# A hybrid decoder step: where the last block's down weights are loaded and split, and how the first block's second norm is put in order

## The chip, the cores and the metric

The kernel runs on one core of a Trainium2 chip. Its engines are TensorE (PE, with PEld for its weight loads), VectorE (DVE), ScalarE (ACT), GpSimd (POOL) and SyncE (SP), which issues the DMAs. The metric is the time of one execution on the device in microseconds (us), as the median of several runs. Lower is better.

## The reference

One layer of a decoder that mixes attention with a spatial gate, on 2048 prompt positions and on 8 sequences of 4 new positions each (the samples). In outline:

```python
z = rmsnorm(x, norm1_g) @ w_in            # 1024 -> q, k, v | u, v of the gate
att  = dilated_window_attention(q, k, v)  # 8 heads, three dilations, merged
gate = spatial_gate(layernorm(vg))        # chunks of 128 positions
x = x + concat(att, u * gate) @ w_out     # 1024 -> 1024
n = rmsnorm(x, norm2_g)
x = x + (silu(n @ w_gate) * (n @ w_up)) @ w_down   # 1024 -> 2816 -> 1024
y = rmsnorm(x, final_g)                   # and caches of the last keys and values
```

Everything is float32. The change lies in the second norm `n` and in the loads of `w_down`.

## The kernel before

**Tiles and blocks.** The prompt is 16 tiles of 128 tokens. A first part of the kernel (up to about 880 us) does the input projection, attention and gate. Behind it come three blocks of tiles: 0 to 5, 6 to 11, and 12 to 15 with the 32 sample rows. Each block does the output projection in two halves of 512 columns, adds the residual (`acc`), takes the second norm and runs the feed-forward part.

**Precision.** A float32 matrix product is made of three fast ones: each operand is split into a high half (ACT copies it to the type `fp32r`) and a low half (POOL or DVE subtract the high half from the source), and PE multiplies high by high, high by low and low by high. `split_sb` (lines 135 and 138) does this for a whole operand; `high` (L1545) and `low_half` (L1549) for the gate and up weights.

**The feed-forward part.** The 2816 hidden columns are 22 slices `f` of 128. For each slice a *unit* of seven products replaces the eight of gate and up (a scheme of the Strassen kind). `product` (L1597) runs one: 4 steps of 3 matmuls over all tokens of the block into a bank `ps_m`, operand `q` of the slice (`op`) against the normed tokens (`xh`, `xl`). The seven weight operands are made from the weights once, in the first block, and kept in DRAM (`ab_d`); the later blocks load them (`load_source`, L1504) into a ring of eight buffers `fr`. In the first block `load_quarter` (L1510) loads the raw quarters and `gained` (L1513) multiplies them with the norm's gain `g2c`.

**The down products.** The hidden values of two slices (an even and an odd one) are kept, and `down_unit` (L1664, matmuls at L1679) multiplies them with the down weights `dw` of both: 24 matmuls of 512 columns for each tile, into `ps_o`. They run within the next even unit, behind its products 3, 4 and 5. The down weights come by `load_down` (L1586, DMA at L1588, 512 KB) into `fd`, which is a single buffer, and by `split_down` into one of two pairs `dw`.

**What sets the order.** The schedule is manual: each engine runs its instructions in the order in which the code writes them, and SP's DMAs too, each waiting where its buffer is not free. `one(u, q)` writes product `q` of a unit and then what is to follow it: `prepare` of the next slice (the low half of operand `q - 1` on POOL, the high half of operand `q` on ACT, the load of source `q` of the slice after it on SP), `roll` (copies of the sample caches from DRAM to DRAM, L1258), and the down weights:

```python
if q == 2 and f:
    load_down(f)
elif q == (5 if f % 2 else 6):
    split_down(f)
```

So a slice's down weights are loaded behind product 2 of its own unit, and split behind product 5 (odd slices) or 6 (even slices). `later(n, fn)` puts a step off until `tick` has been called `n` times; products, halves of projection and `down_unit` tick.

**The first block's second norm.** `first_block` writes the second halves of the output projection for the tiles in the order 2, 0, 1, 3, 4, 5 (`second_unit`, L1373 to L1375, into `ps_o`). Behind each, `second_end` adds it to the residual and starts the norm: square and sum on ACT (`norm2_a`), one and two ticks later the root, the inverse root by a Newton step on DVE and the scaled copy `xn` on ACT (`norm2_b`), and 1 to 3 ticks after that `norm2_c`: eight transposes on PE into two banks (`norm2_t`, L1439, by default `ps_t`), copies and six sums and differences (`norm2_v`, `norm2_s`), and the split into `xh` and `xl`. In the later blocks `chain` (L1481) writes these steps of a tile together, with the previous tile's `norm2_v` and `norm2_s` in the gaps. The first unit of a block (slice 0) runs in two parts, tiles 0 to 3 and then the rest (`part = 4`). `s1`, printed as `s`, holds a tile's sum and root; `acc` of two numbers are two tiles.

Of the kernel before, what the change touches and what calls it, by code (L numbers as in the profile page):

```python
# [10 lines left out]
F32 = mybir.dt.float32  # L11
# [53 lines left out]
def hymba_step(ctx: ExitStack, tc: tile.TileContext, A: dict, O: dict):  # L65
# [1315 lines left out]
    def out_end(B, i, half, ps):  # L1381
        hs = slice(half * 512, (half + 1) * 512)
        if B.rows[i] == P:
            dve.tensor_add(B.acc[i][:, hs], B.acc[i][:, hs], ps)
        else:
            tmp = zn_tile()[0:SR]
            act.activation(tmp, ps[SR:2 * SR, :], AF.Copy)
            dve.tensor_add(B.acc[i][0:SR, hs], B.acc[i][0:SR, hs], ps[0:SR])
            dve.tensor_add(B.acc[i][0:SR, hs], B.acc[i][0:SR, hs], tmp)
# [90 lines left out]

    def chain(B, i, ps, ahead):  # L1481

        out_end(B, i, 1, ps)
        s1 = B.s1.pop(i)
        act.activation(place_of(B, i)[0][:, 4:8], B.acc[i][:, 512:1024].rearrange("p (s t) -> p s t", t=P), AF.Square,
                       accum_out=s1[:, 3:4])
        rms_b(s1, P, s1[:, 3:4])
        if ahead:
            sums = norm2_v(B, *ahead)
        r = rms_c(s1, P)  # L1490
        xn = square_tile()
        act.activation(xn, B.acc[i], AF.Copy, scale=r)
        if ahead:
            norm2_s(B, *ahead, sums)
        return xn
# [16 lines left out]

    def gained(f, q):  # L1513
        w_ = ab[f]["q", q]
        for k in range(4):
            kk = k + (0, 0, 4, 4)[q]
            act.activation(w_[:, k * P:(k + 1) * P], w_[:, k * P:(k + 1) * P], AF.Copy, scale=g2c[:, kk:kk + 1])
        j = (0, 3, 6, 2)[q]
        if j != 3:
            ab[f][j] = w_  # L1520
# [385 lines left out]
    def second_end(B, i, ps, put_off=2):  # L1906
        out_end(B, i, 1, ps)
        norm2_a(B, i, put_off)

    def first_block(B):  # L1910

        m2, m1 = acc_place(2), acc_place(4)
        split_early(B, 1, m1)
        split_early(B, 2, m2)
        B.place()
        load_cat(B, 0, KD - 1, KD)
        load_cat(B, 5, 0, KD)
        merge_load(h, 2)
        load_acc(B, 1)
        load_acc(B, 0)  # L1920
        half1_load(*range(KD))
        sync.dma_start(gain[0], dap(A["final_g"], 0, [[0, P], [1, D]]))
        plan.run(10 ** 9)
        split_early(B, 3)
        for n, what in ((2, [(merge, h, 2, pool), (merge, h, 3, pool), (split_cat, B, 0), (split_early, B, 4)]),
                        (4, [(merge_store, h, 2, 4)]), (5, [(open_end, B, 1)]),
                        (6, [(half1_split, B, 0, 1)]), (7, [(open_end, B, 0), (split_cat, B, 5)]),
                        (8, [(half1_split, B, 2, 3)]), (9, [(half1_split, B, 4, 5), (sources, B, 0, 0, 1, 2, 3)]),
                        (10, [(half1_split, B, 6, 7)]), (11, [(sources, B, 1, 0, 1, 2, 3)])):
            later(n, both, *what)  # L1930
        for i in (1, 2, 3):
            open_unit(B, i)
        open_part(B, 0, (KD - 1,), False, True)
        for i in (4, 5):
            open_unit(B, i)
        first_operands(B)

        p2 = second_unit(B, 2)
        for i in (2, 3):
            load_acc(B, i)  # L1940
        second_end(B, 0, second_unit(B, 0))
        open_end(B, 2)
        second_end(B, 2, p2, 3)
        p1 = second_unit(B, 1)
        for i in (4, 5):
            load_acc(B, i)
        second_end(B, 1, p1)
        p3 = second_unit(B, 3)
        open_end(B, 3)
        second_end(B, 3, p3)  # L1950
        for i in (4, 5):
            open_end(B, i)
        for i in (4, 5):
            second_end(B, i, second_unit(B, i), 1)

    def first_end(B, i):
        open_end(B, i)
# [51 lines left out]
    for bi, B in enumerate(blocks):  # L2009
        if bi == 0:  # L2010
            first_block(B)
        else:
            next_block(B, downs, finals)
        if B.last:
            hs4 = consts.tile([P, 4, 2 * SR], F32R, name="hs4", tag="cats")
        nb = None if B.last else blocks[bi + 1]

        part = 4
        units = [dict(f=f, a=0, b=B.nt) for f in range(NF)]
        if not B.last:  # L2020
            units[0:1] = [dict(f=0, a=0, b=part), dict(f=0, a=part, b=B.nt)]
        rows = list(range(len(B.rows)))
        last_h = {}

        def one(u, q):
            tick()
            product(B, u, q)
            f = u["f"]
            if u["b"] < B.nt:
                if bi == 0 and q in (0, 2):  # L2030
                    sources(B, 2, q, q + 1)
                return

            if f and q < 2:
                prepare(B, f, 7 + q)
            if f + 1 < NF:
                prepare(B, f + 1, q)
            if f + 2 < NF:
                if bi == 0 and f:
                    if q in (0, 2):  # L2040
                        sources(B, f + 2, q, q + 1)
                if bi == 0:
                    ahead_of(f + 2, q)
            elif nb:

                for s in {(0, 2): (0, 1), (0, 4): (2, 3), (1, 3): (4, 5), (1, 5): (6, 7)}.get((f + 2 - NF, q), ()):
                    load_wo(0, s, fraw)
                if f + 1 == NF and q > 0:
                    split_wo(nb, 0, q - 1, lambda s: op_tile())
            if f + 1 < NF and q in (1, 3, 5)[:(1, 3, 2)[bi]]:  # L2050
                roll(1)

            if q == 2 and f:
                load_down(f)
            elif q == (5 if f % 2 else 6):
                split_down(f)

        def downs_of(pair, a, b):
            for i in rows[a:b]:
                down_unit(B, i, pair)  # L2060

        for n, u in enumerate(units):
            u["n"] = n
            for q in range(7):
                one(u, q)
                if u["f"] % 2 == 0 and u["f"] > 0 and 3 <= q < 6:
                    downs_of((B.h[0], B.h[1]), *((0, 2), (2, 4), (4, 9))[q - 3])
        pair = (B.h[0], B.h[1])
# [112 lines left out]
```

## Time and profile before

| | |
|---|---|
| median of three runs | 2521.73 us (2508.28, 2521.73, 2523.93) |
| the profiled execution | 2527.26 us; its span in the trace 2525.4 us |
| granted TensorE clock, mean | 0.989 |
| PE / PEld busy | 2442.6 us (97%) / 2116.0 us (84%) |
| DVE / ACT / POOL busy | 1270.2 (50%) / 1130.9 (45%) / 1303.2 us (52%) |
| DMA | 365.07 MB read, 157.84 MB written, 207 GB/s over the span |

The span is the time from the first to the last instruction in the trace of one execution; the rest of that execution's time lies around it. Busy shares are of the span. Rows of a timeline begin with the start in us, the length in us and the engine; then come the line of the kernel, the operation, its output and input, and "xN" where N like instructions are drawn together. A bracket at the end tells how long the engine stood idle ahead of the instruction, and which instruction's end released it. "SPq" is the DMA queue of SP, where a row's start is the issue; a row of "DMA" is a transfer. The granted clock is the share of full speed that the chip allows TensorE.

### The profile page before, as it was taken

The numbers are of one execution on the slowest core, as the hardware profiler recorded it, in microseconds if no ns is written. First come the engines' busy times: TensorE is split into PE (matmuls) and PEld (weight loads), VectorE is DVE, ScalarE is ACT, GpSimd is POOL, SyncE is SP. The second block draws the span as 40 slices with busy tenths as digits, with TensorE's granted clock in tenths as the row PEclk, the third lists the DMA queues.
The fourth block names the chain that finished last, engine by engine and source line by source line (L and its number), as shares of the span: only waits on it lengthen the run. The fifth ranks groups of instructions, "written<-read, shape, count | busy, mean of one in ns | idle before, by whom it ended". The sixth has DMA issues, their size and how long they took to land.

```text
span 2525.4 us, 39104 instructions
## 1 busy us (share of the span) xinstructions
PE 2442.6 (97%) x14022; PEld 2116.0 (84%) x14022; DVE 1270.2 (50%) x2595; ACT 1130.9 (45%) x2449; POOL 1303.2 (52%) x1019
## 2 busy tenths in 40 slices
PE   8998999999999899999999999999999998999997
PEld 7877776668887678999999989999999978888986
DVE  4558582217776645444444465444444465444444
ACT  7324343226666556454554446233233255333334
POOL 2216441005778447676776626445355445556565
PEclk9999999999999899999999999999999999999999
DMA  9974845675554554555555363535445363555553
GB/s 294 280 230 148 259 127 175 200 253 175 182 168 131 142 191 154 167 175 179 155 194 166 128 218 134 188 136 199 170 169 203 117 223 126 175 200 178 197 174 132
DMA packets 292292, 455.36 MB, mean 180 GB/s; under 512 B 28711, under 2 KB 160984, under 8 KB 286980
## 3 DMA queue, kind: packets, MB, share of 16 engines
q1 hardware_dynamic: 285252, 440.82, 53.6%
q10 hardware_dynamic: 6848, 12.06, 1.7%
q8 instruction: 111, 1.82, 0.3%
q14 instruction: 81, 0.66, 0.1%
HBM read 365.07 MB, written 157.84 MB: 207 GB/s over the span
## 4 chain that ended last, share of the span: by engine, by line
PE 62%; POOL 6%; issue 6%; DVE 3%; DMA 3%; ACT 2%; SPq 0%; POOLq 0%; DVEq 0%; ACTq 0%
PE ps_o L1679 15%; PE ps_m L1608 9%; PE ps_m L1607 9%; PE ps_m L1606 9%; POOL op L1549 4%; PE ps_s L856 3%; PE ps_o L911 2%; PE ps_t L883 1%; PE ps_s L935 1%; PE ps_s L318 1%; PE ps_o L1373 1%; PE ps_o L1375 1%; PE ps_o L1374 1%; PE ps_m L1373 1%; PE ps_m L1375 1%
## 5 line engine op out<-in xcount | busy, mean ns | idle before, releaser
L1549 POOL TENSOR_TENSOR op<-fr,op 128x512 fp32r<-128x512 f32 x385 | 487.5, 1299 | 246.6 <-ACT op L1545 232.5
L1606 PE MATMUL ps_m<-xh,op 128*128 128x384 f32 (+3 forms) x1904 | 604.9, 318 | 0.7 <-DVE zn L1627 0.4
L1608 PE MATMUL ps_m<-xh,op 128*128 128x384 f32 (+3 forms) x1904 | 604.4, 317 | 0.0
L1607 PE MATMUL ps_m<-xl,op 128*128 128x384 f32 (+3 forms) x1904 | 603.9, 317 | 0.1
L1679 PE MATMUL ps_o<-dw,hw 128*128 128x512 f32 x2040 | 492.6, 396 | 20.4 <-POOL dw L138 12.6
L1679 PEld LDWEIGHTS ps_o<-dw,hw 128*128 128x128 f32 x2040 | 385.1, 190 | 106.3 <-POOL dw L138 16.5
L1606 PEld LDWEIGHTS ps_m<-xh,op 128*128 128x128 f32 x1904 | 360.2, 189 | 5.3 <-ACT xh L1450 0.7
L1607 PEld LDWEIGHTS ps_m<-xl,op 128*128 128x128 f32 x1904 | 360.0, 189 | 4.0 <-DVE xl L1462 0.4
L1681 DVE TENSOR_TENSOR acc<-acc,ps_o 128x512 f32<-128x512 f32 (+1 forms) x362 | 248.3, 687 | 226.8 <-PE ps_o L1679 226.8
L1608 PEld LDWEIGHTS ps_m<-xh,op 128*128 128x128 f32 x1904 | 359.9, 189 | 0.0
L1646 ACT ACTIVATE ps_t<-zn 128x384 f32<-128x384 f32 (+1 forms) x126 | 58.5, 465 | 500.7 <-DVE zn L1629 423.8
L138 POOL TENSOR_TENSOR dw<-fd,dw 128x1024 fp32r<-128x1024 f32 x66 | 158.5, 2401 | 204.2 <-ACT dw L135 194.0
L1545 ACT ACTIVATE op<-fr 128x512 fp32r<-128x512 f32 x396 | 233.8, 626 | 3.4 <-PE ps_m L1375 3.4
L318 PE MATMUL ps_s<-wh,xh 128*128 128x512 f32 x480 | 196.8, 410 | 6.0 <-ACT xh L135 6.0
L320 PE MATMUL ps_s<-wh,xl 128*128 128x512 f32 x480 | 189.0, 394 | 0.0
L319 PE MATMUL ps_s<-wl,xh 128*128 128x512 f32 x480 | 188.9, 394 | 0.0
L1549 POOL TENSOR_TENSOR op<-pair,op 128x512 fp32r<-128x512 f32 x63 | 81.3, 1298 | 113.7 <-ACT op L1545 109.3
L536 POOL TENSOR_TENSOR pr<-kv,qb 96x512 f32<-96x512 f32 x32 | 45.6, 1425 | 170.3 <-DMA kv<-in_cache_k_dram 86.1
L318 PEld LDWEIGHTS ps_s<-wh,xh 128*128 128x128 f32 x480 | 90.9, 189 | 48.5 <-issue 23.7
L1656 ACT ACTIVATE hw<-ps_t 128x384 fp32r<-128x384 f32 (+1 forms) x126 | 54.2, 449 | 157.7 <-DVE ps_t L1652 157.7
L927 POOL CAST sq<-k 128x512 fp32r<-128x512 f32 x32 | 34.1, 1066 | 164.8 <-PE ps_s L319 164.8
L1274 DVE TENSOR_TENSOR hw<-ps_t,hw 128x384 fp32r<-128x384 f32 (+1 forms) x120 | 59.3, 508 | 109.7 <-ACT hs L1660 57.0
(490 smaller groups left out, 4328.7 us busy)
## 6 DMA issues: line engine op xcount, KB each, us to landing
fr<-ab_d SPq DMA_DIRECT2D x308, 256.0 KB
fd<-in_w_down_dram SPq DMA_DIRECT2D x66, 512.0 KB
out_ks_dram<-in_cache_k_dram SPq DMA_DIRECT2D x56, 512.0 KB
out_vs_dram<-in_cache_v_dram SPq DMA_DIRECT2D x56, 512.0 KB
ab_d<-fr SPq DMA_DIRECT2D x88, 256.0 KB
qk_d<-pair SPq DMA_DIRECT2D x64, 256.0 KB
ab_d<-pair SPq DMA_DIRECT2D x63, 256.0 KB
kv<-in_cache_k_dram SPq DMA_DIRECT2D x64, 192.0 KB
```

The costliest lines, as they stand in the source:

```text
L138: (eng_lo or pool).tensor_sub(lo, src, hi.bitcast(F32))
L318: pe.matmul(o[j], xh[:, k, :], wh, start=(k == 0), stop=False)
L319: pe.matmul(o[j], xh[:, k, :], wl, start=False, stop=False)
L320: pe.matmul(o[j], xl[:, k, :], wh, start=False, stop=(k == KD - 1))
L856: pe.matmul(s[:, a:b_], d[q][:, qs], d["k"][:, t0:t0 + b_ - a], start=(z == 0), stop=(z == 1))
L1545: act.activation(ops[f, j][0], ab[f][j], AF.Copy)
L1549: (pool if f or j in POOL_LOW else dve).tensor_sub(lo_, ab[f][j], hi.bitcast(F32))
L1606: pe.matmul(out, wh[:, ks], xh[:, :, k], start=(k == 0), stop=False)
L1607: pe.matmul(out, wh[:, ks], xl[:, :, k], start=False, stop=False)
L1608: pe.matmul(out, wl[:, ks], xh[:, :, k], start=False, stop=(k == 3))
L1679: pe.matmul(ps[0:nr], l_, r_[:, cs], start=(z == 0 and y == 0), stop=(z == FC - 1 and y == len(pairs) - 1))
L1681: dve.tensor_add(B.acc[i][0:nr, cs], B.acc[i][0:nr, cs], ps[0:nr])
```

## The change

In the last block, the split of an odd slice's down weights moves from behind product 5 to behind product 3 of its unit, that of an even slice stays behind product 6, and the load of the next slice's down weights is written directly behind each split, where it was behind product 2 of the slice's own unit. In the first block, the norm steps put off by ticks are replaced by `chain`, in a written order of projections, chains and transposes; tiles 2 and 3 transpose into banks of `ps_m`, tiles 4 and 5 into banks of `ps_o`; the root's activation table is loaded by a small activation at the front; the first unit runs in parts of three tiles each; and the gain of the quarters of slices 0 and 1 is one multiplication on POOL in place of four activations on ACT. `part` in the second block stays 4.

```diff
     def chain(B, i, ps, ahead):
-        out_end(B, i, 1, ps)
-        s1 = B.s1.pop(i)
-        act.activation(place_of(B, i)[0][:, 4:8], B.acc[i][:, 512:1024]..., AF.Square,
-                       accum_out=s1[:, 3:4])
-        rms_b(s1, P, s1[:, 3:4])
+        if ps is not None:
+            out_end(B, i, 1, ps)
+        if i in B.s1:
+            ...
+        else:
+            s1 = fl.tile([P, 4], F32, name="s1", tag="s1", bufs=6)
+            act.activation(place_of(B, i)[0], B.acc[i]..., AF.Square, accum_out=s1[:, 0:1])
+            rms_b(s1, P)
...
     def gained(f, q):
         w_ = ab[f]["q", q]
-        for k in range(4):
+        if f < 2:
+            kk = (0, 0, 4, 4)[q]
+            w3 = w_.rearrange("p (k c) -> p k c", k=4)
+            pool.tensor_mul(w3, w3, g2c[:, kk:kk + 4].unsqueeze(2).broadcast_to([P, 4, P]))
+        for k in range(4 if f > 1 else 0):
             kk = k + (0, 0, 4, 4)[q]
             act.activation(w_[:, k * P:(k + 1) * P], w_[:, k * P:(k + 1) * P], AF.Copy, scale=g2c[:, kk:kk + 1])
...
+        two = lambda fn, *a: [lambda: fn(*a[0:1]), lambda: fn(*a[1:2])]
         p2 = second_unit(B, 2)
+        act.activation(fl.tile([P, 4], F32, name="s1", tag="s1", bufs=6)[:, 0:1], ident[:, 0:1], AF.Sqrt)
         for i in (2, 3):
             load_acc(B, i)
-        second_end(B, 0, second_unit(B, 0))
+        p0 = second_unit(B, 0)
         open_end(B, 2)
-        second_end(B, 2, p2, 3)
+        out_end(B, 2, 1, p2)
+        x0 = chain(B, 0, p0, None)
+        x2 = chain(B, 2, None, None)
         p1 = second_unit(B, 1)
         for i in (4, 5):
             load_acc(B, i)
-        second_end(B, 1, p1)
+        open_end(B, 3)
+        x1 = chain(B, 1, p1, (0, norm2_t(B, 0, x0)))
         p3 = second_unit(B, 3)
-        open_end(B, 3)
-        second_end(B, 3, p3)
         for i in (4, 5):
             open_end(B, i)
-        for i in (4, 5):
-            second_end(B, i, second_unit(B, i), 1)
+        x3 = chain(B, 3, p3, (2, norm2_t(B, 2, x2, two(ps_m, 1, 2))))
+        p4 = second_unit(B, 4)
+        x4 = chain(B, 4, p4, (1, norm2_t(B, 1, x1)))
+        p5 = second_unit(B, 5)
+        x5 = chain(B, 5, p5, (3, norm2_t(B, 3, x3, two(ps_m, 1, 2))))
+        later(3, norm2_c, B, 4, x4, two(ps_o))
+        later(5, norm2_c, B, 5, x5, two(ps_o))
...
-        part = 4
+        part = 4 if bi else 3
...
-            if q == 2 and f:
+            if B.last:
+                if q == (3 if f % 2 else 6):
+                    split_down(f)
+                    if f + 1 < NF:
+                        load_down(f + 1)
+            elif q == 2 and f:
                 load_down(f)
             elif q == (5 if f % 2 else 6):
                 split_down(f)
```

The order on SP in the middle of the last block. `fr` are the sources of the operands, `fd` the down weights, and the rows of 16x8192 a cache copy. Before:

```order
L1258 DMA out_vs_dram<-in_cache_v_dram 16x8192
L1504 DMA fr<-ab_d 128x512
L1588 DMA fd<-in_w_down_dram 128x1024
L1504 DMA fr<-ab_d 128x512
L1258 DMA out_vs_dram<-in_cache_v_dram 16x8192
L1504 DMA fr<-ab_d 128x512 x5
```

Of the change, from the end of an even unit to behind the split in the odd unit after it:

```order
L1258 DMA out_vs_dram<-in_cache_v_dram 16x8192
L1510 DMA fr<-ab_d 128x512 x3
L1598 DMA fd<-in_w_down_dram 128x1024
L1510 DMA fr<-ab_d 128x512 x2
L1258 DMA out_vs_dram<-in_cache_v_dram 16x8192
L1510 DMA fr<-ab_d 128x512 x2
L1258 DMA out_vs_dram<-in_cache_v_dram 16x8192
L1598 DMA fd<-in_w_down_dram 128x1024
L1510 DMA fr<-ab_d 128x512 x5
```

A load of `fd` stood behind the third source load of every unit. Now the odd slice's load stands ahead of all seven of its unit's source loads (behind product 6 of the even unit), and the next even slice's load behind product 3 of the odd unit, with three source loads of that unit still to come.

The order on ACT over a pair of slices of the last block: `op` are the high halves of the gate and up operands, `dw` the high half of the down weights, `zn` the first copy of a unit's product 0, `ps_t` the SiLUs, `hw` and `hs` the hidden values. Before:

```order
L135 ACTIVATE dw<-fd 128x1024
L1616 ACTIVATE zn<-ps_m_23601 128x272
L1545 ACTIVATE op<-fr 128x512 x2
L1646 ACTIVATE ps_t_23656<-zn 128x272
L1545 ACTIVATE op<-fr 128x512 x3
L1646 ACTIVATE ps_t_23720<-zn 128x272
L1545 ACTIVATE op<-fr 128x512
L135 ACTIVATE dw<-fd 128x1024
L1656 ACTIVATE hw<-ps_t_23720 128x4x64
L1660 ACTIVATE hs_20687<-ps_t_23720 128x16
```

Of the change:

```order
L135 ACTIVATE dw<-fd 128x1024
L1626 ACTIVATE zn<-ps_m_23580 128x272
L1555 ACTIVATE op<-fr 128x512 x2
L1656 ACTIVATE ps_t_23635<-zn 128x272
L1555 ACTIVATE op<-fr 128x512 x2
L135 ACTIVATE dw<-fd 128x1024
L1555 ACTIVATE op<-fr 128x512
L1656 ACTIVATE ps_t_23702<-zn 128x272
L1555 ACTIVATE op<-fr 128x512
L1666 ACTIVATE hw<-ps_t_23702 128x4x64
L1670 ACTIVATE hs_20665<-ps_t_23702 128x16
```

The odd slice's `dw` stood directly ahead of the hidden values; now two high halves and the second SiLU of the unit stand between them. POOL's `dw` moves with it: six low halves stood between the even slice's and the odd slice's, and now four.

In the first block, the order on ACT around the norms of tiles 0 and 2 (`s` their sums and roots, `xh` the place to which the square is written, `pair` the normed tile). Before:

```order
L1418 ACTIVATE xh_9102,s_9403<-acc_9112 128x1024
L1418 ACTIVATE xh_9102,s_9407<-acc_9366 128x1024
L1545 ACTIVATE op<-raw 128x512
L1545 ACTIVATE op<-fr 128x512
L1395 ACT_TABLE_LOAD
L1395 ACTIVATE s_9403<-s_9403 128x1
L1395 ACTIVATE s_9407<-s_9407 128x1
L1545 ACTIVATE op<-fr 128x512
L1545 ACTIVATE op<-raw 128x512
L1426 ACTIVATE pair<-acc_9112,s_9403 128x1024
L1426 ACTIVATE pair<-acc_9366,s_9407 128x1024
```

Of the change:

```order
L1950 ACT_TABLE_LOAD
L1950 ACTIVATE s_9354<-ident 128x1
L1492 ACTIVATE xh_9102,s_9395<-acc_9112 128x1024
L1395 ACTIVATE s_9395<-s_9395 128x1
L1498 ACTIVATE pair<-acc_9112,s_9395 128x1024
L1492 ACTIVATE xh_9102,s_9405<-acc_9356 128x1024
L1395 ACTIVATE s_9405<-s_9405 128x1
L1498 ACTIVATE pair<-acc_9356,s_9405 128x1024
L1555 ACTIVATE op<-raw 128x512
```

A tile's square, root and scaled copy stood apart with high halves between them; now those of one tile stand together, ahead of the high halves.

PE at the last projection and the first products of that block (L1375 the projection, L1439 transposes, L1606 to L1608 and L1616 to L1618 the products). Before:

```order
L1375 MATMUL ps_o_9642<-wol,xl_9103 128x512
L1439 MATMUL ps_t_9707<-ident,pair 128x128 x4
L1439 MATMUL ps_t_9712<-ident,pair 128x128 x4
L1606 MATMUL ps_m_9734<-xh_9102,op 128x256
L1607 MATMUL ps_m_9734<-xl_9103,op 128x256
```

Of the change:

```order
L1375 MATMUL ps_o_9631<-wol,xl_9103 128x512
L1439 MATMUL ps_m_9657<-ident,pair 128x128 x4
L1439 MATMUL ps_m_9662<-ident,pair 128x128 x4
L1616 MATMUL ps_m_9693<-xh_9102,op 128x192
L1617 MATMUL ps_m_9693<-xl_9103,op 128x192
```

The transposes ahead of the first product go to two banks of `ps_m` in place of `ps_t`, and the first product has 3 tiles x 64 columns in place of 4 x 64.

More of the change, by code (lines that the diff above doesn't have):

```diff
@@ L1481, in chain @@
     def chain(B, i, ps, ahead):
-        out_end(B, i, 1, ps)
-        s1 = B.s1.pop(i)
-        act.activation(place_of(B, i)[0][:, 4:8], B.acc[i][:, 512:1024].rearrange("p (s t) -> p s t", t=P), AF.Square,
-                       accum_out=s1[:, 3:4])
-        rms_b(s1, P, s1[:, 3:4])
+        if ps is not None:
+            out_end(B, i, 1, ps)
+        if i in B.s1:
+            s1 = B.s1.pop(i)
+            act.activation(place_of(B, i)[0][:, 4:8], B.acc[i][:, 512:1024].rearrange("p (s t) -> p s t", t=P), AF.Square,
+                           accum_out=s1[:, 3:4])
+            rms_b(s1, P, s1[:, 3:4])
+        else:
+            s1 = fl.tile([P, 4], F32, name="s1", tag="s1", bufs=6)
+            act.activation(place_of(B, i)[0], B.acc[i].rearrange("p (s t) -> p s t", t=P), AF.Square, accum_out=s1[:, 0:1])
+            rms_b(s1, P)
         if ahead:
```

## The prediction

> **What bounds the kernel now.** I read the page's busy times first, then the list of waits of each engine in the last block, then the timeline at the places where TensorE (PE) waits, then the same microseconds on the engines that it waits for.
>
> ```profile
> PE 2442.6 (97%) x14022; PEld 2116.0 (84%) x14022; DVE 1270.2 (50%) x2595; ACT 1130.9 (45%) x2449; POOL 1303.2 (52%) x1019
> ```
>
> PE is busy for 97% of the span. The change neither adds nor removes a matmul, so it can only win back what PE loses by waiting or by a lower granted clock. The waits of the last block (us in total, times, longest):
>
> ```profile
> PE ps_o L1679 <- POOL dw L138: 11.6, 10, 1.3
> PE ps_o L1679 <- ACT hw L1656: 4.5, 6, 1.2
> ...
> ACT dw L135 <- DMA fd<-in_w_down_dram: 52.7, 10, 6.2
> ...
> SPq L1504 <- POOL op L1549: 261.4, 132, 14.2
> ```
>
> Ten times, once for each pair of hidden slices, the down products (L1679) wait for the down weights of the pair's second, odd slice. Behind that stands ACT, which waits ten times for their load (fd), 5.3 us on average. The last row is the DMA queue's: its source loads run in step with POOL, each waiting for a buffer that a low half frees. The timeline of PE shows a group of 24 down products that is undisturbed, then one that waits:
>
> ```profile
> 2150.59 5.63 PE L1679 MATMUL ps_o<-dw,hw 128*128 128x512 f32 x24
> 2156.06 0.29 PE L1606 MATMUL ps_m<-xh,op 128*128 128x272 f32 x1
> ...
> 2157.56 1.98 PE L1679 MATMUL ps_o<-dw,hs 128*64 128x512 f32 x8
> ...
> 2177.53 0.86 PE L1679 MATMUL ps_o<-dw,hw 128*128 128x512 f32 x3
> 2178.90 0.50 PE L1679 MATMUL ps_o<-dw,hw 128*128 128x512 f32 x1 [0.52 <-ACT hw L1656]
> 2180.73 6.43 PE L1679 MATMUL ps_o<-dw,hw 128*128 128x512 f32 x20 [1.33 <-POOL dw L138]
> ```
>
> Undisturbed, 24 take 2156.06 - 2150.59 = 5.47 us, and a product of 12 gate and up matmuls takes 1.50 (to 2157.56). I laid one window over each of the ten waiting groups (stretch, length, PE busy, PEld busy, clock, DMA share, GB/s):
>
> ```profile
> 2177.53:2187.00 9.47, 7.62 (x24) 5.38 (x24) 0.82 0.56 176
> ...
> sum 83.20, PE 66.98 PEld 47.90; mean PE 6.70 PEld 4.79
> ```
>
> The ten last 83.20 us instead of 54.7: **28.5 us too long**. Only 16.1 of that is waiting (11.6 + 4.5); the other 12.4 is the clock, 0.82 in this group, and the restart behind each gap.
>
> **The last block, worked out.** The pair of 2160 to 2181 on ACT, POOL and the DMA queue, and two windows (DVE, ACT, POOL busy, clock, DMA share, GB/s at the end). The odd slice's unit starts at about 2161.0: its seven products and four of the next unit precede 2177.53.
>
> ```profile
> 2162.90 1.06 ACT L135 ACTIVATE dw<-fd 128x1024 fp32r<-128x1024 f32 x1
> 2164.04 2.40 POOL L138 TENSOR_TENSOR dw<-fd,dw 128x1024 fp32r<-128x1024 f32 x1 [3.48 <-ACT dw L135]
> 2170.61 0.42 SPq L1588 DMA_DIRECT2D fd<-in_w_down_dram  x1
> 2177.17 1.06 ACT L135 ACTIVATE dw<-fd 128x1024 fp32r<-128x1024 f32 x1 [5.59 <-DMA fd<-in_w_down_dram]
> ...
> 2160.00:2170.00 10.00, 10.00 (x82) 10.00 (x81) 4.61 (x13) 5.71 (x13) 6.51 (x5) 1.00 0.19 54
> 2170.00:2180.00 10.00, 8.88 (x65) 8.09 (x64) 2.93 (x9) 3.78 (x10) 5.62 (x5) 1.00 0.85 289
> ```
>
> The even slice's split ends on POOL at 2166.44, but the odd slice's load is issued only at 2170.61, behind source loads and a cache copy, and lands 6.6 us later. ACT stands in front of it for 5.59 us with the hidden conversions (hw) queued behind, and both waits of PE come from there. The change issues the load right behind the even split, at about 2166.5: 4.1 us earlier, with the DMA engines 19% busy. The DMA queue now waits there for POOL's split; queued behind it are the next source loads, which wait for low halves that POOL runs after the split anyway, so nothing is late by it.
>
> How long the load takes with nothing ahead of it, the trace doesn't show. The nearest rows from both sides are a 256 KB load, from its issue to the instruction that it frees, and a loaded 512 KB one:
>
> ```profile
> 1013.93 0.52 SPq L1510 DMA_DIRECT2D fr<-in_w_up_dram  x1
> 1017.19 1.30 POOL L1549 TENSOR_TENSOR op<-pair,op 128x512 fp32r<-128x512 f32 x1 [4.39 <-DMA fr<-in_w_up_dram]
> 2317.92 7.21 DMA fd<-in_w_down_dram
> ```
>
> So 3.3 to 7.2 us. I take 4.2, near the lower row because the queue is nearly empty: 3.3 plus another 256 KB at the 289 GB/s of the busy window. Then it lands at 2170.7, ACT takes 1.06 and POOL 2.4, and the weights are ready at 2174.3; PE wants them three matmuls into the group, at 2178.2. **That wait goes, with 3.9 us to spare.** What is late next: the split moves from behind product 5 to behind product 3, so on POOL it stands ahead of the low halves of the next unit's operands 3 and 4. Low half 3 takes 1.30 more and ends at 2166.5 + landing + 4.8; product 3 starts at 2176.0 and wants it two matmuls later, at 2176.2. With 4.2 us that is 0.7 to spare: **from a landing of 4.9 us on, PE waits there**. ACT, held until 2171.8, then has the activation of product 5 and the conversions, which took 1.9 us behind the even unit (2161.0 to 2162.9); with some 1.5 us of queued work they end near 2175.3, ahead of 2177.5. For what I don't see I leave a quarter microsecond a pair: 28.5 - 2.5 = **-26 us**, with 0 and -28.5 as bounds.
>
> [...]
>
> **The first block, worked out.** Four stages (PE, PEld, DVE, ACT, POOL busy, clock): the second halves of the output projection with the norm, the part-unit of four tiles, that of two, and the second unit with the products up to the down weights. Then three starts on PE.
>
> ```profile
> 903.90:952.86 48.96, 40.76 (x186) 32.92 (x184) 25.60 (x66) 32.10 (x70) 16.09 (x13) 0.93 0.48 157
> 952.86:966.64 13.78, 12.73 (x95) 12.52 (x94) 8.43 (x24) 8.33 (x18) 6.95 (x6) 0.88 0.00 0
> 966.64:975.98 9.34, 9.34 (x87) 9.34 (x85) 4.73 (x11) 6.36 (x19) 6.36 (x6) 1.00 0.32 115
> 975.98:1000.91 24.93, 24.02 (x138) 23.46 (x137) 9.96 (x18) 17.28 (x44) 23.33 (x18) 1.00 0.65 205
> ...
> 916.91 0.50 PE L1373 MATMUL ps_o<-woh,accm 128*128 128x512 f32 x1 [1.98 <-DVE acc L1384]
> 936.09 1.09 PE L1439 MATMUL ps_t<-ident,pair 128*128 128x128 f32 x4 [3.47 <-DVE zn L1463]
> 959.37 0.37 PE L1606 MATMUL ps_m<-xh,op 128*128 128x256 f32 x1
> ```
>
> The new order adds tile 2 ahead of tile 0, so tile 1's products find their bank free and the 1.98 us go (if tile 2's residual has landed). The gap of 3.47 does not simply go, for each tile's norm is now one chain through DVE and ACT:
>
> ```profile
> 943.53 0.69 DVE L1384 TENSOR_TENSOR acc<-acc,ps_o 128x512 f32<-128x512 f32 x1 [0.55 <-PE ps_o L1375]
> 945.44 0.15 DVE L1394 TENSOR_SCALAR s<-s 128x1 f32<-128x1 f32 x1 [1.22 <-ACT xh L1418]
> 956.14 0.20 ACT L1395 ACTIVATE s<-s 128x1 f32<-128x1 f32 x1
> 957.32 1.15 ACT L1426 ACTIVATE pair<-acc,s 128x1024 f32<-128x1024 f32 x1 [0.71 <-DVE s L146]
> ...
> 925.92 0.39 ACT L1450 ACTIVATE xh<-ps_t 128x256 fp32r<-128x256 f32 x1
> 928.41 0.68 DVE L1468 TENSOR_TENSOR xl<-ps_t,xh 128x512 fp32r<-128x512 f32 x1
> 928.78 2.54 POOL L138 TENSOR_TENSOR xl<-zn,xh 128x512 fp32r<-128x512 f32 x2 [2.03 <-ACT xh L135]
> ```
>
> From the add to the normed tile is 2.06 + 2.33 = 4.4 us; from the first copy of its transpose the banks are free after 3.2 us and the tile is split after 5.4. Following the new order by hand: tile 0 is normed at 914.9 + 4.4 = 919.3, tile 2, whose chain stands behind it on ACT, at 923. From there one tile's add follows the other's by square, root, copies and six subtractions, some 6 us, and 8 where four more DVE instructions stand between: the adds of tiles 1, 3, 4 and 5 end near 925.7, 934, 940.4 and 946.1. PE has its last transposes but two done at 940.3, then stands: the first product's bank holds tile 3's transposes, whose copies stand behind tile 5's square on ACT, and is free at 946.1 + 3.3 = 949.4. Against 952.86 that is 3.5 us earlier, behind a gap of 9 us. Behind the gap of 3.47 us the clock fell, too: the 0.93 of that stage is 3.4 us, the 0.88 of the next 1.7, and so much I charge the first part-unit again.
>
> ```profile
> 962.13 2.55 POOL L138 TENSOR_TENSOR xl<-zn,xh 128x512 fp32r<-128x512 f32 x2 [3.88 <-ACT xh L135]
> ...
> 998.47 2.39 POOL L138 TENSOR_TENSOR dw<-fd,dw 128x1024 fp32r<-128x1024 f32 x1 [0.36 <-ACT dw L135]
> ...
> 1000.91 1.42 PE L1679 MATMUL ps_o<-dw,hw 128*128 128x512 f32 x5 [0.91 <-POOL dw L138]
> ...
> L997 POOL TENSOR_TENSOR sm<-st,sel_g 128x256 f32<-128x256 f32 x7 | 4.4, 626 | 4.3 <-ACT e L867 4.3
> ```
>
> Halves of three tiles are nothing: 84 matmuls of 128 columns take 9.34 us (0.111 each), 60 of 256 take 966.64 - 959.37 (0.121); 168 of 192 lie between 18.7 and 20.4 against 19.5. Then POOL decides. It splits tile 5 until 964.68, and from there its queue runs to the down weights at 1000.86, for which PE waits. In the new order tile 5's copies stand behind an activation table load and a SiLU, and its split ends at 965 to 966.4; but up to 4 of the 4.6 us in which POOL pauses between 966.64 and 1000.91 can close, so the down weights come at 996.6 to 1001. The eight gain multiplications that move from ACT to POOL, 1.25 us each by the row with a broadcast operand (twice 0.626), lie ahead of tile splits, where POOL waits for ACT anyway; without that cover they cost up to 5 us. So -4 to 0, and +4 where a chain is longer than I follow it; I take **-2 us**.
>
> **Sum.** The profiled execution took 2527.26 us (span 2525.4 and 1.9 around it): 2527.3 - 26 - 2 = 2499.3. It is 5.5 us above the median of 2521.73; on the median that is **2494 us**.
>
> **Rivals.**
> - *The clock does not come back.* Only the 16.1 us of waits and the 2 in front go: 2504. [...] Against: the windows between the groups have 1.00. 15%.
> - *The load lands late.* At 5.5 to 7.2 us the wait moves to product 3, 0.6 to 2.3 us a pair; at the upper end 23 of the 28.5 stay: 2516. For it: the two fd rows above took 6.6 and 7.2. Against: they had transfers ahead of them. 14%.
> - *The first block loses.* The gap of 9 us and POOL's longer queue cost 4 instead of giving 2: 2500. 8%.
> - *Slower.* In the odd unit, ACT's queue stands at the earlier split. If the load, though first, lands 7.7 us or more after its issue (4.9 plus the 2.8 that a pair loses today), product 3 waits more than the down products did. At 10 us: 10 x 5.1 - 28.5 = +22, 2544. Against: 19% DMA share at the issue. 6%.
>
> The forecast has 57%, its own range is 2487 to 2501. About 1% (2496.5) is what a measurement of this kernel tells from no change; some three quarters of the forecast's share lie below it, the first three rivals lie within 1%, and only the last is slower by more: faster 0.42, same 0.52, slower 0.06. The range 2486 to 2519 takes in all but the slower case and the ends.
>
> **What would show it.** ACT's wait for fd gone, the ten groups at 5.5 us with the clock at 1.00, and no wait of the gate and up products for POOL. In the first block one PE gap of some 9 us ahead of the first part-unit, and the first down products through at 997 to 1001. I am wrong if product 3 waits for a low half, if the clock still dips without waits, or if the first block comes out more than 4 us shorter.

## The result, and the profile after

The changed kernel takes **2498.99 us** (median of 7 runs, 2493.89 to 2503.05) against 2521.73 us (median of 7, 2508.28 to 2531.99): a ratio of 0.9907, with a 95% interval of 0.988 to 0.9935. Forecast were 2494 us, within 2486 to 2519. The profiled execution of the changed kernel took 2501.57 us, its span is 2499.7, 25.7 less than before. The page's busy times, and the waits of PE from the last block's projections to its end (us in total, times, longest):

```profile
PE 2431.1 (97%) x14022; PEld 2111.0 (84%) x14022; DVE 1270.9 (51%) x2595; ACT 1123.1 (45%) x2418; POOL 1310.3 (52%) x1027
...
PE ps_t L1439 <- ACT pair L1498: 3.5, 1, 3.5
PE ps_o L1689 <- DVE acc L1691: 1.5, 1, 1.5
PE ps_t L1439 <- ACT xns L1426: 1.1, 1, 1.1
```

The matmuls are the same 14022, and in the last block none waits for the down weights (`dw`) or the hidden values (`hw`) any more. To see where the 25.7 us come from I laid two windows over either trace: from the first matmul of the first block's second projections to the down products that wait for slice 1's weights, and from the last block's first product to its last rows (stretch, length, busy times, clock, DMA share, GB/s). Before:

```profile
903.90:1000.91 97.01, 86.85 (x497) 78.25 (x495) 48.72 (x118) 64.07 (x148) 52.73 (x41) 0.95 0.44 143
2107.50:2499.50 392.00, 375.65 (x2408) 341.53 (x2409) 176.71 (x388) 143.65 (x324) 235.96 (x170) 0.97 0.53 181
```

After:

```profile
906.09:1004.29 98.20, 84.26 (x497) 76.69 (x495) 55.72 (x119) 59.11 (x129) 58.91 (x46) 0.95 0.42 136
2110.85:2474.06 363.21, 363.08 (x2411) 336.30 (x2409) 176.09 (x388) 146.02 (x324) 236.07 (x171) 0.99 0.57 195
```

The last block is 28.8 us shorter, and PE is busy in it from end to end (363.08 of 363.21). The first block's stage is 1.2 us longer. It also begins 2.2 us later; in the traces of this case, with the old or the new order behind it, this start lies anywhere between 899.5 and 906.1 us.

The pair of slices in the last block that corresponds to the one followed in the prediction, on the DMA queue, ACT, POOL and PE:

```profile
2163.53 0.33 SPq L1598 DMA_DIRECT2D fd<-in_w_down_dram  x1
2167.14 1.06 ACT L135 ACTIVATE dw<-fd 128x1024 fp32r<-128x1024 f32 x1 [2.49 <-DMA fd<-in_w_down_dram]
2168.45 2.39 POOL L138 TENSOR_TENSOR dw<-fd,dw 128x1024 fp32r<-128x1024 f32 x1
2174.59 5.65 PE L1689 MATMUL ps_o<-dw,hw 128*128 128x512 f32 x24
```

The load is issued when the even split ends, lands 3.6 us later (3.4 to 4.2 over the ten pairs), and the weights are split at 2170.84, 3.8 us before the group that wants them starts. ACT still stands 2.49 us in front of the load (over the last block 29.8 us in 11 waits, where it was 52.7 in 10), but PE waits for nothing that stands behind it. The ten groups, each with its own window as before, the last column but two the clock:

```profile
2174.59:2180.08 5.49, 5.49 (x24) 4.32 (x24) 1.00 1.03 333
...
sum 54.90, PE 54.89 PEld 43.21; mean PE 5.49 PEld 4.32
```

All ten last 5.49 us with the clock at 1.00: 54.9 in place of 83.2.

### The profile page after: what moved, and what is told of

Same layout as the page of the kernel before. It is cut to its first block, busy times and chain, and to the rows that moved or that the text cites. A ratio compares the mean times of both kernels' runs of the same rounds, so it can differ in the third digit from the quotient of the medians.

```text
span 2499.7 us, 39079 instructions
## 1 busy us (share of the span) xinstructions
PE 2431.1 (97%) x14022; PEld 2111.0 (84%) x14022; DVE 1270.9 (51%) x2595; ACT 1123.1 (45%) x2418; POOL 1310.3 (52%) x1027
## 4 chain that ended last, share of the span: by engine, by line
PE 73%; DVE 3%; ACT 2%; POOL 1%; issue 1%; DMA 1%; SPq 0%; DVEq 0%; ACTq 0%; POOLq 0%
PE ps_o L1689 19%; PE ps_m L1616 11%; PE ps_m L1618 11%; PE ps_m L1617 11%; PE ps_s L856 2%; PE ps_o L911 2%; PE ps_t L883 1%; PE ps_s L935 1%; PE ps_s L318 1%; PE ps_m L1373 1%; PE ps_s L320 1%; PE ps_s L319 1%; PE ps_m L1375 1%; PE ps_m L1374 1%; PE ps_o L1373 1%
## 5 line engine op out<-in xcount | busy, mean ns | idle before, releaser
L1616 PE MATMUL ps_m<-xh,op 128*128 128x384 f32 (+4 forms) x1904 | 604.8, 318 | 10.6 <-DVE zn L1463 9.3
L1618 PE MATMUL ps_m<-xh,op 128*128 128x384 f32 (+4 forms) x1904 | 604.4, 317 | 1.6 <-POOL op L1559 1.6
L1617 PE MATMUL ps_m<-xl,op 128*128 128x384 f32 (+4 forms) x1904 | 603.9, 317 | 0.1
L1689 PE MATMUL ps_o<-dw,hw 128*128 128x512 f32 x2040 | 480.5, 391 | 3.9 <-DVE acc L1691 3.3
L1616 PEld LDWEIGHTS ps_m<-xh,op 128*128 128x128 f32 x1904 | 360.3, 189 | 15.2 <-ACT xh L1453 9.5
L1618 PEld LDWEIGHTS ps_m<-xh,op 128*128 128x128 f32 x1904 | 360.0, 189 | 2.0 <-POOL op L1559 2.0
L320 PEld LDWEIGHTS ps_s<-wh,xl 128*128 128x128 f32 x480 | 90.9, 189 | 20.5 <-POOL xl L138 0.4
```

Source lines behind the costliest of these rows:

```text
L320: pe.matmul(o[j], xl[:, k, :], wh, start=False, stop=(k == KD - 1))
L1616: pe.matmul(out, wh[:, ks], xh[:, :, k], start=(k == 0), stop=False)
L1617: pe.matmul(out, wh[:, ks], xl[:, :, k], start=False, stop=False)
L1618: pe.matmul(out, wl[:, ks], xh[:, :, k], start=False, stop=(k == 3))
L1689: pe.matmul(ps[0:nr], l_, r_[:, cs], start=(z == 0 and y == 0), stop=(z == FC - 1 and y == len(pairs) - 1))
```

## Experiments

**Each part alone.** The first kernel is the one before with the last block's part of the diff alone; the second is the changed kernel with the old rule in all blocks:

```diff
-            if B.last:
-                if q == (3 if f % 2 else 6): ...
             if q == 2 and f:
                 load_down(f)
             elif q == (5 if f % 2 else 6):
                 split_down(f)
```

> The kernel before with the last block's part of the change alone (load of the next slice's down weights behind each split, odd split behind product 3). Theory: the whole gain sits here. In the change's trace the last block, from its first product to its first last-rows product, is 28.8 us shorter; so 2521.7 - 29 = 2493 us, ratio 0.9885, the ten groups of down products at 5.5 us without a wait, and the first block as before (97.0 us from its second projections to the first down products that pass). Rival: the two parts share the gain (the medians are only 22.7 us apart): 2504 to 2510 us.

> The change without its last-block part (the first block's new order alone). Theory: the first block gives nothing, its stage is 98.2 us in the change's trace against 97.0 before, since POOL's queue sets its end: 2521 to 2525 us, ratio 1.000 to 1.002, and the last block as before, ten groups of 83 us. Rival, the prediction's own term: 2 us faster; rival two, the first block takes part in the gain: ratio 0.995 or lower.

Measured: the last block's part alone 2499.41 us, ratio 0.9913 (0.9895 to 0.9932); the first block's part alone 2518.88 us, ratio 0.9999 (0.9983 to 1.0016). So the gain sits in the last block, a little less than the 2493 us forecast and far from the rival's 2504 to 2510. The first block's part shows no gain; its interval, some 4 us to either side, can't tell 2 us from nothing, and the stages in the traces must. The windows of the last block's part alone, first block and last block:

```profile
899.54:998.30 98.76, 86.95 (x497) 77.91 (x496) 48.72 (x118) 64.36 (x148) 52.84 (x41) 0.95 0.44 141
2104.73:2467.34 362.61, 362.35 (x2408) 335.67 (x2409) 176.26 (x388) 145.99 (x324) 236.61 (x171) 1.00 0.58 196
```

and those of the first block's part alone:

```profile
902.82:1001.62 98.80, 84.24 (x498) 76.78 (x496) 55.75 (x119) 59.53 (x129) 60.29 (x47) 0.95 0.42 138
2108.22:2489.70 381.48, 368.35 (x2411) 336.46 (x2410) 176.69 (x388) 143.67 (x324) 236.13 (x170) 0.99 0.54 186
```

Two things were not expected. The old first block is 97.0 us in one trace and 98.8 in the other, so the 1.2 us above are no difference; with the new order it is 98.2 to 99.5 in five traces. No gain of 2 us shows there. And the old last block takes 381.5 us here, not 392.0: its loss is not a constant. This kernel's waits of PE in the last block, and the windows over its ten groups, show why:

```profile
PE ps_o L1689 <- POOL dw L138: 10.6, 10, 1.3
...
PE ps_o L1689 <- ACT hw L1666: 2.4, 4, 1.1
...
2174.16:2180.93 6.77, 5.77 (x24) 4.25 (x24) 1.00 0.43 130
2209.39:2217.34 7.95, 6.03 (x24) 4.24 (x24) 1.00 0.33 107
...
2421.88:2431.87 9.99, 7.62 (x24) 5.37 (x24) 0.83 0.42 146
...
sum 73.34, PE 60.33 PEld 43.55; mean PE 6.03 PEld 4.35
```

One group of ten has a clock below 1.00. In the trace of before there are four, the one shown in the prediction and these:

```profile
2137.79:2149.07 11.28, 8.82 (x24) 6.29 (x24) 0.70 0.54 168
...
2287.22:2296.41 9.19, 7.64 (x24) 5.41 (x24) 0.81 0.56 174
2324.87:2334.89 10.02, 7.54 (x24) 5.35 (x24) 0.83 0.56 167
```

**Is it the load or the split?** The change moves both. Three kernels put one of them elsewhere: the odd split behind product 5 or 6 with the loads left early, and the load back behind product 2 with the split left behind product 3.

```diff
-                if q == (3 if f % 2 else 6):
+                if q == (5 if f % 2 else 6):     # second kernel: if q == 6:
```

```diff
-            if B.last: ...
-            elif q == 2 and f:
+            if q == 2 and f:
                 load_down(f)
-            elif q == (5 if f % 2 else 6):
+            elif q == ((3 if B.last else 5) if f % 2 else 6):
                 split_down(f)
```

> The change, with the odd slices' split put back behind product 5 in the last block (the loads still directly behind the splits). Theory: the early issue of the load is what wins, not the earlier split; with the load landed 3.6 us after its issue the split ends on POOL about 1 to 2 us later than in the change and still ahead of the down products: same time as the change, 2498 us (ratio 0.990 to 0.992), groups of 5.5 us. Rival: the split's earlier place is needed, and waits of 0.5 to 1.3 us come back in most groups: 2505 to 2515 us.

> The change, with the odd slices' split behind product 6 in the last block, so that it stands behind the hidden values on ACT and two low halves later on POOL. Theory: the split ends near 2174.9 on the change's clock of time, and the third matmul of the group wants it at 2175.3: no wait or one of a few tenths, same time as the change or up to 5 us more. Rival: it comes late in every pair by a low half (1.3 us), and with the restarts that costs 15 to 20 us.

> The change, with the loads of the last block put back behind product 2 of the slice's own unit, while the odd slices' split stays behind product 3. Theory: an earlier split without an earlier load is worse than nothing: ACT stands in front of the load from product 3 on, some 9 us instead of 5.6, with a SiLU, two high halves and the hidden values behind it, so the hidden values come 3 to 4 us later than before: 30 to 40 us over the kernel before, 2550 to 2560 us. Rival: the split alone is harmless, as the load lands at the same time either way: as before, 2520 us.

Measured: split behind product 5, 2501.59 us, ratio 0.9924 (0.9904 to 0.9943); behind product 6, 2502.17, ratio 0.9929 (0.9911 to 0.9946); late load with early split, 2569.31, ratio 1.0189 (1.0166 to 1.0212). The last block's windows of the first two kernels:

```profile
2110.98:2473.96 362.98, 362.85 (x2410) 336.08 (x2409) 177.48 (x388) 143.63 (x324) 235.74 (x170) 0.99 0.58 195
```

```profile
2108.91:2472.00 363.09, 362.96 (x2411) 336.11 (x2410) 177.41 (x388) 144.85 (x323) 235.73 (x170) 0.99 0.58 195
```

Both are 363 us, as with the change: within that window the place of the split is indifferent, and **the early issue of the load is the whole effect**. One wait came with the split behind product 6, outside the window: at 2477.04 us the down products of the last rows (L1705) stand 1.90 us for `dw`, which they do not with the split behind product 3 or 5. The third kernel's waits of PE in the last block, and ACT's for the load, show the price of the split without the load:

```profile
PE ps_m L1616 <- ACT hs L1670: 29.3, 9, 4.6
PE ps_m L1618 <- POOL op L1559: 11.8, 10, 1.4
...
ACT dw L135 <- DMA fd<-in_w_down_dram: 94.1, 11, 10.3
```

ACT stands in front of the load for longer, 8.6 us a time in place of 5.3, and the products themselves wait for what is queued behind. The direction was as forecast; the 50 us are 10 more than the upper end.

**What a wait costs.** A kernel with early loads, but with the odd split written so late that PE must wait:

```diff
             if B.last:
-                if q == (3 if f % 2 else 6): ...
+                if f % 2 == 0 and f and q == 2:
+                    split_down(f - 1)
+                    load_down(f)
+                elif q == 6 and f % 2 == 0:
+                    split_down(f)
+                    load_down(f + 1)
+                elif f == NF - 1 and q == 3:
+                    split_down(f)
```

> The change, with the odd slices' split written behind product 2 of the next even unit, so that the down weights are late on purpose although their load is early; one wait of about 3 us in each of the ten groups, and no wait of ACT for the load. It measures what a PE wait costs beyond itself. By the rows of before and of the kernel with the first block's change alone, a wait costs 0.3 to 0.6 us of restart, and where the clock falls 2 us more, in 4 and in 1 of ten groups. Theory: the clock falls in most groups at this longer wait: 10 x (3 + 0.5 + 2) = 55 us over the change, 2553 us, granted clock 0.7 to 0.85 in the groups. [...]

Measured: 2539.39 us, ratio 1.0071 (1.0048 to 1.0093), 40 us over the change. Its waits of PE in the last block, and three of its groups:

```profile
PE ps_o L1689 <- POOL dw L138: 21.8, 10, 2.9
PE ps_o L1689 <- ACT dw L135: 2.7, 10, 0.3
...
2179.33:2189.35 10.02, 7.64 (x24) 5.37 (x24) 0.83 0.91 294
2217.81:2229.06 11.25, 8.89 (x24) 6.31 (x24) 0.70 0.90 311
...
2409.39:2417.82 8.43, 6.05 (x24) 4.24 (x24) 1.00 0.94 318
...
sum 97.78, PE 73.29 PEld 51.82; mean PE 7.33 PEld 5.18
```

The waits are about 2.4 us in each group and not 3, and the clock falls in seven of ten. The theory is right that it falls; the total of 40 us is 15 below its 55.

What a wait costs beyond itself can be read from the groups whose clock stayed at 1.00. Undisturbed, PE is busy for 5.49 us; with one wait it is 5.75 to 5.78, with two 6.03 to 6.07. So each wait costs about 0.27 us more, the restart. A group with two waits whose clock falls is busy for 7.64 us (the one at 2179.33) where it would be 6.05. In windows of half a microsecond the group of before at 2177.53 has a clock of 1.00 up to 2181.5, of 0.50 from 2182.0 to 2185.0, and of 1.00 again from 2185.5. The clock lost there is 0.18 x 9.47 = 1.7 us, so it stood at half speed for 3.4 us; where a group's clock is 0.70 it was twice as long (0.50 from 2141.0 to 2147.5 in the one of before at 2137.79). With this the loss of three kernels' ten groups against 54.9 us splits up as follows:

| | loss | waits | restarts | what is left: the clock |
|---|---|---|---|---|
| before | 28.3 | 16.1 (16) | 4.3 | 7.9 (5 falls in 4 groups) |
| first block's part alone | 18.4 | 13.0 (14) | 3.8 | 1.6 (1 fall) |
| odd split behind product 2 of the next unit | 42.9 | 24.5 (20) | 5.4 | 13.0 (9 falls in 7 groups) |

(Waits and their number from the lists; restarts at 0.27 us each; a stretch of 3.4 us at half speed is one fall, and one of twice that counts as two.) So a fall costs 1.4 to 1.6 us. Of these 30 groups, the ten with less than 1.5 us of waits all kept the full clock; of the twenty with 1.5 to 3.2 us, twelve fell and eight did not.

No single wait of these groups is over 2.9 us, and groups with the same 2.4 us of waits came out at 1.00 and at 0.83 (of the three shown above, those at 2409.39 and 2179.33). What decides between the two the runs do not show.

**The first block: what sets its end.** The changed first block has one PE gap of 9.3 us, ahead of the first part-unit, whose bank tile 3's transposes still hold:

```profile
PE ps_m L1616 <- DVE zn L1463: 9.3, 1, 9.3
```

One kernel begins the products in another bank, the next also moves the sums of slice 1's operands to DVE, the last also moves the split of slice 0's down weights forward:

```diff
         part = 4 if bi else 3
+        if bi == 0:
+            turn[3] = 2
...
-        d, eng = ab[f], pool if f else dve          # second and third kernel
+        d, eng = ab[f], pool if f > 1 else dve
...
+                if bi == 0 and q == 6:              # third kernel, part-unit 1
+                    split_down(0)
                 return
-            elif q == (5 if f % 2 else 6):
+            elif q == (5 if f % 2 else 6) and (f or bi):
```

> The change, with the first block's products beginning in another bank of ps_m, so that the first two do not wait for the transposes of tile 3. Theory: the PE gap of 9.3 us shrinks to 1 to 4 us, the transposes of tiles 4 and 5 come 4 us earlier, POOL's split of tile 5 ends that much earlier, and the stage falls from 98.2 to about 94 to 95 us, PE's own clock in the first units rising from 0.90; time 2495 us against 2499 for the change (ratio to before 0.989). Rival: POOL's queue behind the split only fills with pauses (2.8 us there now), and the stage stays at 97 to 98 us.

> As the kernel with the other first bank, and the five sums of slice 1's operands on DVE in place of POOL (POOL 1.3 us each, 6.5 us in all, DVE 0.7 each). Theory: POOL sets when the second slice's down weights are split, so the stage falls by another 2 to 3 us, until PE's own work binds it (units of 24 us without a wait): 91.5 to 93 us, time 2492 to 2493 us. Rival: ACT's queue (the high halves, gains and copies) binds as well, and the sums move nothing: as the kernel with the bank alone.

> As the kernel with the other first bank and the sums on DVE, and the split of slice 0's down weights moved from behind slice 0's last product to the end of the first part-unit, where POOL waits for ACT (7.5 us of pauses there between tile 5's split and 976 us in that kernel's trace). Theory: with the sums on DVE POOL has idle time, but in the wrong place, ahead of its queue of low halves; moved there, 2.4 us of POOL's work leave the stretch that ends with slice 1's down weights, and PE's wait of 1.7 us for a low half behind that split goes: stage 92 to 92.5 us against 94.4, time 2 us less. Rival: ACT's queue binds (its own dw copy moves too), and the stage stays at 94 us.

Measured: 2494.11 us, ratio 0.9887 (0.9869 to 0.9905); 2495.64, ratio 0.9896 (0.9878 to 0.9913); 2495.33, ratio 0.9903 (0.9887 to 0.992). Against the changed kernel these differences are within the intervals: none of the three is shown to be faster. Only the stage in the traces can tell more. POOL's split of tile 5, its split of slice 1's down weights and PE's first down products behind it, of the change:

```profile
967.06 2.52 POOL L138 TENSOR_TENSOR xl<-zn,xh 128x512 fp32r<-128x512 f32 x2 [2.34 <-ACT xh L135]
1001.84 2.40 POOL L138 TENSOR_TENSOR dw<-fd,dw 128x1024 fp32r<-128x1024 f32 x1 [0.37 <-ACT dw L135]
1004.29 4.87 PE L1689 MATMUL ps_o<-dw,hw 128*128 128x512 f32 x20 [0.65 <-POOL dw L138]
```

and of the kernel with the other bank (its second projections begin at 902.39, those of the change at 906.09):

```profile
959.34 2.52 POOL L138 TENSOR_TENSOR xl<-zn,xh 128x512 fp32r<-128x512 f32 x2 [2.33 <-ACT xh L135]
994.67 2.39 POOL L138 TENSOR_TENSOR dw<-fd,dw 128x1024 fp32r<-128x1024 f32 x1 [0.36 <-ACT dw L135]
902.39:997.12 94.73, 85.75 (x498) 77.29 (x496) 55.75 (x119) 59.31 (x129) 61.75 (x49) 0.96 0.45 147
```

Measured from there, tile 5's split ends at 59.5 in place of 63.5, the down weights come at 94.7 in place of 98.2: 4.0 us earlier become 3.5, as the theory has it. POOL's queue behind the last tile sets the end of this stage; PE's gap matters as far as it puts that tile off. The stages of the other two are 0.4 and 1.1 us shorter, less than forecast:

```profile
903.34:997.71 94.37, 85.34 (x497) 77.15 (x495) 57.49 (x123) 59.30 (x129) 57.95 (x46) 0.96 0.46 150
904.92:998.16 93.24, 85.79 (x497) 77.26 (x496) 58.37 (x123) 59.30 (x129) 56.93 (x44) 0.92 0.46 148
```

The third kernel's trace is no fair measure: its granted clock is 0.941 over the whole span, about 0.05 below the others from start to end, where its three other executions have 0.990 to 0.992. In the second the rival is seen: relieved of the sums, POOL waits for ACT's high halves instead, 2.15 and 2.67 us ahead of the first operands of slice 1:

```profile
964.95 1.29 POOL L1559 TENSOR_TENSOR op<-fr,op 128x512 fp32r<-128x512 f32 x1 [2.15 <-ACT op L1555]
968.91 1.30 POOL L1559 TENSOR_TENSOR op<-pair,op 128x512 fp32r<-128x512 f32 x1 [2.67 <-ACT op L1555]
```

**Two details of the new first block**, each put back alone: the parts of four and two tiles (`part = 4`), and the gains on ACT (`gained` as before for all slices).

> The change, with the first block's first unit in parts of four and two tiles as before. Theory: the first product then needs tile 3's split as well, which POOL ends 2 to 4 us after the bank is free, and its own parts cost the same (84 matmuls of 256 and 84 of 128 columns against 168 of 192); tile 5's split comes 1 to 3 us later, and the stage from the second projections to the first down products that pass is 100 to 102 us against 98.2 to 99.5 in the five traces with the change's first block. Rival: the bank sets the start for both, and the stage stays at 98 to 99.5 us.

> The change, with the gains of slices 0 and 1 back on ACT (32 activations of 0.31 us, 10 us in all) and off POOL (8 of about 1.1 us). Theory: those of slice 1 stand within the chains of tiles 1, 3 and 5 on ACT and put tile 5's split off by 2 to 4 us: stage 100 to 102 us. Rival: POOL's queue was what they lengthened, and the stage is shorter than 98 us; rival two: both are covered, 98 to 99.5 us.

Measured: 2498.7 and 2499.91 us, one execution each, so that only the stage can be compared. It is, of the first kernel and of the second:

```profile
903.14:1001.52 98.38, 84.58 (x497) 77.24 (x495) 54.40 (x119) 59.27 (x129) 59.26 (x46) 0.95 0.42 136
```

```profile
901.63:1002.61 100.98, 84.39 (x497) 76.92 (x495) 54.70 (x118) 65.37 (x150) 54.70 (x41) 0.93 0.43 138
950.99 0.50 PE L1616 MATMUL ps_m<-xh,op 128*128 128x192 f32 x1 [11.19 <-DVE zn L1463]
```

The halves of three tiles are worth nothing (98.4, among 98.2 to 99.5 in the traces of the change's first block): the bank, not tile 3's split, sets the start (the first product waits 9.26 us for the same DVE row as in the change). The gains on POOL are worth 1.5 to 2.8 us of the stage, by this one trace: on ACT they stand within the chains of the tiles, and the first product starts 49.4 us behind the second projections in place of 47.4.

## Why the prediction was right, and where it was off

- *The load that comes late to ACT is the cause of both waits of PE.* Shown: with the load early, the waits of the ten groups are gone whether the split stands behind product 3, 5 or 6; with the load late, the early split makes it worse. One sign that was named did not come: ACT's own wait for `fd` is not gone, it fell from 52.7 to 29.8 us. By the prediction's own sum, in which ACT is held until 2171.8, it had to stay; what went is that PE waits behind it.
- *A landing of 4.2 us, a limit of 4.9.* It was 3.4 to 4.2 us over the ten pairs, and product 3 waits for no low half. The allowance of a quarter microsecond a pair was not needed: the last block's windows differ by 28.8 us, where -26 was forecast; the bound of -28.5 was right to 0.3.
- *The clock comes back without the waits.* Shown by the ten groups at 1.00. The rival that it would not is refuted; the late split shows the reverse, with falls in seven groups.
- *The scaling to the median was off.* The 5.5 us by which the profiled execution lay above its median were taken off the sum, and the whole 28.5 us besides. But some 8 us of the 28.5 are falls of the clock, in four groups of that execution and in one of the kernel that has the same last block, whose profiled execution was 9.8 us shorter, and its last block 10.5. So a part of those 5.5 us was very likely the same loss, counted twice; how much, the runs do not show, as the other executions of before have no trace. The changed kernel's profiled execution lay only 2.6 us above its own median. The old order's executions lie between 2508 and 2532 us, the change's between 2494 and 2503. The median fell by 22.7 us, the profile by 25.7.
- *The first block, -2 us: no gain* (0.9999, 0.9983 to 1.0016; the stage 98.2 to 99.5 us against 97.0 and 98.8). The step that failed is the end of tile 5's split on POOL. Forecast were 965 to 966.4, which is 61.1 to 62.5 us behind the second projections; it was 63.5, as the first product started at 47.4 and not at 45.5: tile 5's add ended at 950.16, 44.1 behind them, not 42.2. Tile 1's add was on time (21.5 behind, forecast 21.8); the 2 us came in behind it, at tile 3's (31.5, forecast 30.1) and tile 4's (38.5, forecast 36.5). There DVE's operand work, which stands ahead of these adds, took more than twice as long as before:

```profile
932.48 1.61 DVE L1548 TENSOR_TENSOR raw<-fr,raw 128x512 f32<-128x512 f32 x1
934.01 1.78 DVE L1559 TENSOR_TENSOR op<-fr,op 128x512 fp32r<-128x512 f32 x1
942.43 1.61 DVE L1559 TENSOR_TENSOR op<-fr,op 128x512 fp32r<-128x512 f32 x1
```

  In the trace of before the like rows take 0.69 us (at 923.31, 923.91 and 932.21), while POOL stands idle. In the new order POOL runs a tile's split or a low half at the same time, and its two tile splits there take longer as well, 2.99 and 2.96 us in place of 2.5. That the two slow each other down is what these rows suggest; no run here tests it. The gap of 9 us came as forecast (9.3), the pauses of POOL closed by 1.9 us (4.6 to 2.7), not by up to 4, and the first down products came 98.2 us behind the second projections, outside the 997 to 1001 that were named (93.1 to 97.1). The gains were costed at nothing, and were worth 2 us or so; the parts of three tiles were costed at nothing, and are.

## What to carry to other kernels

A load into a single buffer should be issued by the step that frees the buffer, ahead of the queue's other work, and not by the step that comes before its use: here this moved no matmul and took 17 to 23 us off the median in the four kernels that compare its parts (2499 to 2502 us). When an engine waits often for the same short time, add to the wait the restart (here 0.27 us) and the clock behind it (here 1.4 to 1.6 us a fall), and treat the clock's part as chance: the number of falls in one traced execution (5 and 1 here, with the same last block) need not be that of the median. When one engine's work is moved to run beside another's, look at the length of their rows again (here 0.69 us became 1.6 to 1.8). When several engines run a chain in order, look for the queue that is busy to the end of the stage (here POOL's) and ask what puts off its last input; shortening the bound engine's gap is worth only that.

## What the runs showed of the hardware

In the last block, PE waits of 0.2 to 2.9 us were followed by a granted clock of half speed for about 3.4 or 6.8 us in 4, 1 and 7 of ten groups (before, first block's part alone, odd split behind product 2 of the next unit), with 1.6, 1.3 and 2.4 us of waits a group on average. The ten groups with less than 1.5 us of waits kept the full clock, the others fell in twelve of twenty cases; each 3.4 us at half speed cost 1.4 to 1.6 us. A wait without a fall cost 0.27 us beyond itself. A 512 KB load issued with little ahead of it reached the engine that waited for it in 3.4 to 4.2 us, where behind source loads and a cache copy it took 6.6. Operand work on DVE took 0.69 us with POOL idle, and 1.6 to 1.8 us in three rows that ran beside POOL's work.
